# Eight rows of 512 bytes instead of 1,024 single words: the row sums of the spatial weights in a decoder step

## The chip, the cores and the metric

The kernel runs on one core of one Trainium2 chip. The metric is the device time of one execution in microseconds (us). The kernel before was timed in three runs: 998.34 us in the median, 995.13 the lowest and 999.16 the highest.

## The reference, cut to what matters

One decoder layer is computed for 1,024 prompt tokens and 8 sample tokens. A large projection `xn @ w_in` gives seven blocks of 1,024 columns: u, v, z_a, x_b, z_b and the gates g_a and g_b. The change is in branch A, which normalises v and mixes it within chunks of 128 tokens, with one lower-triangular matrix of 128x128 for each of eight groups of channels:

```
u = gelu(u)
vn = layernorm(gelu(v), ln_g, ln_b)                  # per token, over 1,024 channels
w = tril(w_s)                                        # (8, 128, 128): h, t, s
s = einsum('hts,bcshd->bcthd', w, vn) + b_s[h, t]    # per chunk c
y_a = u * s * silu(z_a)
```

The kernel takes gain and bias of the layer norm out of the mixing. With v' the normalised v ahead of gain and bias, channel d of group h has

```
s[t, d] = ln_g[d] * sum_s w[h, t, s] v'[s, d]  +  ln_b[d] * rowsum[h, t]  +  b_s[h, t]
rowsum[h, t] = sum_s w[h, t, s]
```

The 1,024 numbers `rowsum` (8 groups by 128 rows) are what the change stores in another way.

## The kernel before, in words

All products run on TensorE (PE) in fp32r, each as three passes over operands that are cut into a high and a low part. A large product is a Strassen scheme of seven products for each pair of output blocks; one of them takes some 2.8 us. ScalarE (ACT) and VectorE (DVE) cut the weights, form the sums of weights that Strassen needs, and take the results out of PSUM. The stages follow each other in the stream of steps: v, gate A (tiles named ga, garaw, gas, gaw), u and z_a, branch B, gate B, the two merges, the output projection and the embedding gate.

Beside the gate A products the kernel finishes v. `v_planes` cuts the words of each of two v blocks into planes (tiles vw) and turns each with a DMA transpose (`v<-vw`, a pair of them in each call, issued by SyncE, SP); `v_join` puts the turned words together on ScalarE (`big<-v`), and `v_turn` applies gelu. The weights of the next pair of gate blocks are loaded by `Weights.fetch` (two DMAs `garaw`, also on SP).

The functions that the change touches, with the profile's line numbers: `ln_loads` (L938) loads `w_s` into tile ws and the layer norm's gain and bias into the first 16 partitions of tile lnvec. `spatial_weights` (L950) makes ws triangular on GpSimd (POOL), lets VectorE sum its rows (tile rowsums, 128 partitions by 8), stores the sums in DRAM as `rowsum` (8 by 128), turns ws on TensorE (bank psw, 8 transposes) and cuts it, and at last turns lnvec (bank lncol, one transpose) and copies the result to the tile lncol. `spatial_offsets` (L970) loads `rowsum` back, broadcast to all partitions (tile off, 512 KB), and forms the offsets from it, lncol and b_s. `spatial_weights` and `v_planes` are recorded behind the first step of gate A, `ln_loads` three steps into the third pair of v, and `spatial_offsets` behind step 8 of the stream that begins with gate A (L1273 to L1295).

The order of the instructions is not that of the text. All calls behind the start are recorded by `Planner` (L56), which makes the order on every engine. Calls of TensorE in a row into the same tile are one operation of the planner. Each operation depends on those that wrote what it reads, or that read what it writes. Due times are passed backwards (`wanted`, L182): an operation of TensorE is due at its place in the stream of matmuls, and any other operation must end before the earliest due time of the operations that need it. `order` (L204) then takes, engine by engine, the operation that can begin first, and among those that can begin at once the one with the earliest due time, the latter being at most 60 us behind the place where it was recorded. An operation may begin at most 14 us ahead of its due time. In this model each DMA has its bytes and a fixed time to land, whatever its pieces, a store costs SP 0.45 us and a DMA transpose 3 us. SP's DMAs are issued in the order that results, and each waits on SP for its own inputs.

Two resources are shared. There are 46 slots in SBUF for the large tiles (`slot`, L330; lnvec, vw, garaw and gaw each take one), and a new tile takes the slot that was let go first; a load wants three more slots free in the planner. There are two PSUM banks for the small products (`bank`, L339), psw, lncol, vt (the sample's v) and smix (the sample's spatial mix) among them.

In the profile nearly all instructions carry line 299, since the planner issues them there; they are told apart by their tiles.

Of the kernel before, what the change touches and what calls it, by code (L numbers as in the profile page):

```python
# [15 lines left out]
P = 128  # L16
D = 1024
NB = D // P
# [282 lines left out]
@with_exitstack  # L301
def tile_hybrid_step(ctx, tc, *args):
    hybrid_step(ctx, tc, *args)


def hybrid_step(
# [7 lines left out]
    nc = tc.nc  # L314
# [15 lines left out]
    def slot(name, shape=(P, T), dt=F32):  # L330
        n_name[0] += 1
        return plan.tile(spool.tile(list(shape), dt, tag="slot", name=f"{name}_{n_name[0]}", bufs=SLOTS,
                                    padded_shape=None), "slot")
# [5 lines left out]
    def bank(name):  # L339
        n_name[0] += 1  # L340
        return plan.tile(bankp.tile([P, 512], F32, tag="bank", name=f"{name}_{n_name[0]}"), "bank")
# [8 lines left out]
    def split(src, hi, lo):  # L350

        nc.scalar.activation(out=hi, in_=src, func=AF.Copy)
        nc.vector.tensor_tensor(out=lo, in0=src, in1=f32(hi), op=ALU.subtract)

    def dma(out, in_, by=None):
        (by or nc.sync).dma_start(out=out, in_=in_)
# [11 lines left out]
    ident = cpool.tile([P, P], F32, tag="ident", name="ident")  # L368
# [6 lines left out]
    nc = plan  # L375
# [163 lines left out]
    class Features:  # L539

        new = staticmethod(lambda: region("acc"))
        sums = (P, 2, WIDE)
# [15 lines left out]
    class Tokens:  # L558
# [4 lines left out]
        sums = (P, 2, HALF)  # L563
# [366 lines left out]
    lnt = {}  # L930
# [7 lines left out]
    def ln_loads():  # L938
        lnt["ws"] = slot("ws", (P, NB, P))
        dma(lnt["ws"], w_s.rearrange("h t s -> t h s"))  # L940
        vec = lnt["vec"] = slot("lnvec", (P, P))
        for i, v in enumerate((ln_g, ln_b)):
            dma(vec[i * NB : (i + 1) * NB, :], v[0].rearrange("(k p) -> k p", p=P))

    def ln_rows():
        lnt["g"] = row_broadcast(ln_g[0], "lng")
# [3 lines left out]
    def spatial_weights():  # L950

        ws = lnt["ws"]
        nc.gpsimd.affine_select(out=ws, in_=ws, pattern=[[0, NB], [-1, P]], compare_op=ALU.is_ge,
                                fill=0.0, base=0, channel_multiplier=1)
        sums = cpool.tile([P, NB], F32, tag="rowsums", name="rowsums")
        nc.vector.tensor_reduce(out=sums, in_=ws, op=ALU.add, axis=mybir.AxisListType.X)
        dma(kept["rowsum"].rearrange("h t -> t h"), sums)
        lnt["wst"] = []
        for h4 in range(0, NB, 4):
            w = slot("wst", (P, 4, 2, P), F32R)  # L960
            ps = bank("psw")
            for i in range(4):
                nc.tensor.transpose(ps[:, i * P : (i + 1) * P], ws[:, h4 + i, :], ident)
            split(ps.rearrange("p (h t) -> p h t", t=P), w[:, :, 0], w[:, :, 1])
            lnt["wst"].append(w)
        ps = bank("lncol")
        nc.tensor.transpose(ps[:, : 2 * NB], lnt["vec"][: 2 * NB, :], ident[: 2 * NB, : 2 * NB])
        nc.vector.tensor_copy(lncol, ps[:, : 2 * NB].rearrange("p (i k) -> p i k", i=2))

    def spatial_offsets():  # L970

        off = lnt["off"] = slot("off", (P, NB, P))
        dma(off, kept["rowsum"].partition_broadcast(P))
        for h in range(NB):
            nc.vector.scalar_tensor_tensor(out=off[:, h], in0=off[:, h], scalar=lncol[:, 1, h : h + 1],
                                           in1=lnt["bs"][:, h * P : (h + 1) * P], op0=ALU.mult, op1=ALU.add)
# [31 lines left out]
    kept = {}  # L1008
# [262 lines left out]


    at(vsteps[2][3], ln_loads)  # L1273
    at(gasteps[0][0], spatial_weights)
    for i, u in enumerate(vusers):

# [54 lines left out]
    p, l, c = gbsteps[2], gbsteps[3], pasteps[0]  # L1331
    turn_over(yaop, l, [*l[1:], c[0]])
    p, l, c = pasteps[2], pasteps[3], pbsteps[0]
# [414 lines left out]
```

## Time and profile before

| | us |
|---|---|
| median of three runs | 998.34 |
| lowest and highest run | 995.13, 999.16 |
| the profiled execution | 996.61 |
| its span, first to last instruction | 994.9 |
| busy TensorE, share of the span | 979.0, 98% |
| busy VectorE | 797.3, 80% |
| busy ScalarE | 523.4, 53% |
| granted TensorE clock, mean | 0.997 |

A row of the timeline has the start in us from the span's start, the duration, the engine, the line, the operation, the tile written and the tiles read, the size, how many such instructions were merged into the row, and in brackets how long the engine stood idle ahead of it and which releaser ended that. SPq is SP's queue: its rows give the time that SP took to issue DMAs, not the time of the transfer. A row of the table of stretches has the stretch, its length, the busy time of TensorE's matmuls (PE) and weight loads (PEld), VectorE, ScalarE and GpSimd, the granted clock, the DMA share (the mean time that a packet was under way on the 16 DMA engines, over 1 where several were at once) and GB/s. A row of waits has the total in us, how often, and the longest.

### The profile page before, as it was taken

Reading aid. Unit: us, or ns where it says so; the run is one execution under the profiler, and the core shown is the slowest. Engines: PE = TensorE matmul, PEld = TensorE weight load, DVE = VectorE, ACT = ScalarE, POOL = GpSimd, SP = SyncE. Lnnn points to the kernel's source line nnn. Section 1 sums busy time; section 2 is a strip of 40 time slices with the busy share of each in tenths; the row PEclk is TensorE's granted clock in tenths of the full one; section 3 lists DMA queues with packets and bytes.
Section 4 is the critical chain, followed back from the end, with each engine's and each line's share of the span. In section 5 each row is a group of like instructions: output and inputs, shape, how many; then the busy total and the mean of one; then the engine's idle time right before and its main releaser. Section 6 shows DMA issues by size and latency. Waiting matters only on the chain. (4 is left out here: it accounts for less than half of the span.)

```text
span 994.9 us, 15991 instructions
## 1 busy us (share of the span) xinstructions
PE 979.0 (98%) x6110; PEld 878.6 (88%) x6110; DVE 797.3 (80%) x1235; ACT 523.4 (53%) x883; POOL 69.5 (7%) x142
## 2 busy tenths in 40 slices
PE   8999999999999999999999999999999999999996
PEld 6889989999999899899999999999999988888885
DVE  5976558877778888979897987697799898769596
ACT  7778977665434434344533343562353364667463
POOL 2000000000000000001000100000000001213111
PEclk9999999999999999999999999999999999999999
DMA  9325483322464354656735176974663552399546
GB/s 337 133 103 119 116 150 128 101 92 65 143 231 177 106 187 163 215 181 233 254 127 179 29 253 217 305 282 138 227 242 122 178 188 64 88 287 361 157 109 190
DMA packets 106666, 173.48 MB, mean 174 GB/s; under 512 B 25503, under 2 KB 65903, under 8 KB 106582
## 3 DMA queue, kind: packets, MB, share of 16 engines
q1 hardware_dynamic: 104222, 164.56, 49.3%
q0 software_dynamic: 2048, 7.37, 4.2%
q8 instruction: 48, 0.79, 0.3%
q10 hardware_dynamic: 320, 0.54, 0.2%
q14 instruction: 28, 0.23, 0.1%
HBM read 114.84 MB, written 53.87 MB: 170 GB/s over the span
## 5 line engine op out<-in xcount | busy, mean ns | idle before, releaser
L299 DVE TENSOR_TENSOR u<-acc,u 128x520 f32<-128x520 f32 (+1 forms) x90 | 62.6, 695 | 38.0 <-PE acc L299 32.9
L299 POOL TENSOR_TENSOR rstd<-ms,mhalf 128x1 f32<-128x1 f32 (+1 forms) x36 | 30.7, 855 | 190.4 <-DVE ms L299 190.3
L299 POOL MEMSET u<- 128x8 f32 x35 | 4.7, 134 | 503.2 <-PE acc L299 251.0
L299 ACT ACTIVATE u<-acc 128x512 f32<-128x512 f32 x39 | 23.3, 596 | 25.7 <-PE acc L299 25.3
L299 ACT ACTIVATE paw<-pas 128x512 fp32r<-128x512 f32 x16 | 10.0, 627 | 30.3 <-DVE pas L299 25.1
L299 ACT ACTIVATE pbw<-pbs 128x512 fp32r<-128x512 f32 x16 | 10.0, 629 | 26.0 <-DVE pbs L299 23.2
L299 DVE TENSOR_TENSOR big<-big 128x1024 f32<-128x1024 f32 (+4 forms) x20 | 23.6, 1216 | 0.0
L299 ACT ACTIVATE big<-mix 128x256 f32<-128x256 f32 x32 | 12.2, 384 | 19.0 <-PE mix L299 17.1
L299 ACT ACTIVATE big<-v 128x1024 uint16<-128x1024 uint16 x16 | 18.5, 1174 | 6.7 <-DMA v<-vw 6.7
L299 PE MATMUL accm<-qh,wpoolw 128*128 128x260 f32 (+1 forms) x96 | 20.9, 319 | 0.0
L299 ACT ACT_TABLE_LOAD x13 | 16.7, 1283 | 7.0 <-PE acc L299 6.0
L299 ACT ACTIVATE zbw<-zbs 128x512 fp32r<-128x512 f32 x16 | 10.1, 628 | 16.4 <-DVE zbs L299 11.6
L299 ACT ACTIVATE gbw<-gbs 128x512 fp32r<-128x512 f32 x16 | 10.0, 625 | 15.5 <-DVE gbs L299 13.5
L299 DVE TENSOR_TENSOR acc<-acc,u 128x512 f32<-128x512 f32 (+1 forms) x16 | 11.1, 697 | 8.4 <-PE acc L299 8.3
L299 ACT ACTIVATE zaw<-zas 128x512 fp32r<-128x512 f32 x16 | 10.0, 630 | 14.6 <-DVE zas L299 9.1
L299 PEld LDWEIGHTS accm<-qh,wpoolw 128*128 128x128 f32 x96 | 15.6, 188 | 1.9
L299 ACT ACTIVATE uw<-us 128x512 fp32r<-128x512 f32 x16 | 10.0, 626 | 13.4 <-DVE us L299 10.8
L299 DVE TENSOR_TENSOR v<-acc,u 128x520 f32<-128x520 f32 (+1 forms) x9 | 6.3, 697 | 13.3 <-PE acc L299 13.3
L299 ACT ACTIVATE gb<-gb 128x1032 f32<-128x1032 f32 (+1 forms) x8 | 6.8, 854 | 18.8 <-DVE gb L299 18.8
L299 DVE TENSOR_TENSOR big<-mix,big 128x256 f32<-128x256 f32 x32 | 12.7, 419 | 4.8 <-ACT big L299 4.3
L299 ACT ACTIVATE vw<-v 128x1024 uint16<-128x1024 uint16 x16 | 16.1, 1045 | 0.5 <-DVE v L299 0.5
L299 PE MATMUL mix<-wst,vh 128*128 128x256 f32 x64 | 15.5, 319 | 0.0
(685 smaller groups left out, 3623.7 us busy)
## 6 DMA issues: line engine op xcount, KB each, us to landing
ga<-ga SPq DMA_DIRECT2D x16, 516.0 KB
gb<-gb SPq DMA_DIRECT2D x16, 516.0 KB
ya<-za SPq DMA_DIRECT2D x8, 516.0 KB
yb<-zb SPq DMA_DIRECT2D x8, 516.0 KB
x<-in_x_prompt_dram SPq DMA_DIRECT2D x8, 512.0 KB
vraw<-in_w_in_dram SPq DMA_DIRECT2D x8, 512.0 KB
e<-e SPq DMA_DIRECT2D x8, 512.0 KB
garaw<-in_w_in_dram SPq DMA_DIRECT2D x8, 512.0 KB
```

Of the source, the lines that this page charges most:

```text
L299: getattr(getattr(self.nc, e), method)(*args, **kwargs)
```

## The change

`sums` is turned by TensorE in the same bank as lnvec, behind it. VectorE copies the eight rows of 128 sums into a second half of the tile lnvec, which becomes 256 columns wide, and from there they are stored as eight contiguous rows. The store moves from ahead of the psw transposes to the end of the function. The load of `rowsum` in `spatial_offsets` is as before.

```diff
     def ln_loads():
         lnt["ws"] = slot("ws", (P, NB, P))
         dma(lnt["ws"], w_s.rearrange("h t s -> t h s"))
-        vec = lnt["vec"] = slot("lnvec", (P, P))
+        vec = lnt["vec"] = slot("lnvec", (P, 2 * P))
         for i, v in enumerate((ln_g, ln_b)):
-            dma(vec[i * NB : (i + 1) * NB, :], v[0].rearrange("(k p) -> k p", p=P))
+            dma(vec[i * NB : (i + 1) * NB, :P], v[0].rearrange("(k p) -> k p", p=P))
...
         nc.vector.tensor_reduce(out=sums, in_=ws, op=ALU.add, axis=mybir.AxisListType.X)
-        dma(kept["rowsum"].rearrange("h t -> t h"), sums)
         lnt["wst"] = []
...
         ps = bank("lncol")
-        nc.tensor.transpose(ps[:, : 2 * NB], lnt["vec"][: 2 * NB, :], ident[: 2 * NB, : 2 * NB])
+        nc.tensor.transpose(ps[:, : 2 * NB], lnt["vec"][: 2 * NB, :P], ident[: 2 * NB, : 2 * NB])
+        nc.tensor.transpose(ps[:NB, P : 2 * P], sums, ident)
         nc.vector.tensor_copy(lncol, ps[:, : 2 * NB].rearrange("p (i k) -> p i k", i=2))
+        turned = lnt["vec"][:NB, P:]
+        nc.vector.tensor_copy(turned, ps[:NB, P : 2 * P])
+        dma(kept["rowsum"], turned)
```

## The prediction

> **What bounds the kernel now.** I read the head of the page first, then what TensorE (PE) waited for, then TensorE's timeline around its one late wait, and from there backwards through ScalarE (ACT), the queue of SyncE (SP) and the DMA engines, until I came to an operation that the change touches.
>
> ```profile
> span 994.9 us, 15991 instructions
> PE 979.0 (98%) x6110; PEld 878.6 (88%) x6110; DVE 797.3 (80%) x1235; ACT 523.4 (53%) x883; POOL 69.5 (7%) x142
> ```
>
> ```profile
> PE acc L299 <- ACT gaw L299: 2.2, 1, 2.2
> PE warm L299 <- POOL ident masks.py:199: 1.9, 1, 1.9
> ```
>
> TensorE is busy for 98% of the span. The second fence is the head of its list of waits (total, times, longest): the second entry is the warm-up at the very start, and the first is one wait of 2.2 us for a cut of gate weights, gaw. So the kernel is bound by TensorE nearly throughout, and a change can shorten it only by taking matmuls away, by removing that wait, or by letting the matmuls run faster.
>
> ```profile
> 124.09 0.39 PE L299 MATMUL acc<-xB11h,gaw 128*128 128x512 f32 x1
> ...
> 126.85 0.41 PE L299 MATMUL acc<-xB22h,vw 128*128 128x260 f32 x2
> ...
> 145.34 0.66 PE L299 MATMUL smix<-ident,sv 8*128 8x8 f32 x8
> 148.19 0.50 PE L299 MATMUL acc<-xB11h,gaw 128*128 128x512 f32 x1 [2.19 <-ACT gaw L299]
> ...
> 152.87 0.40 PE L299 MATMUL acc<-xB22h,gaw 128*128 128x260 f32 x2
> ```
>
> The first product of the second pair of gate weights should begin when the smix transposes end, at 146.00, and begins at 148.19. It also runs slowly: the same product of the first pair took 126.85 - 124.09 = 2.76 us, this one 152.87 - 148.19 = 4.68 us, 1.92 us more. The last of the stretches below shows why: the granted clock, 1.00 before, is 0.71 from 148 to 150.
>
> ```profile
> 116.00:118.00 2.00, 2.00 (x19) 2.00 (x18) 0.00 (x0) 1.58 (x6) 0.00 (x0) 1.00 1.12 209
> 134.00:136.00 2.00, 2.00 (x10) 1.61 (x9) 1.52 (x6) 2.00 (x5) 0.00 (x0) 1.00 0.78 152
> 136.00:138.00 2.00, 2.00 (x15) 1.87 (x14) 0.97 (x3) 1.97 (x4) 0.54 (x1) 1.00 1.44 68
> 138.00:140.00 2.00, 2.00 (x17) 1.95 (x16) 1.40 (x2) 0.22 (x1) 0.00 (x0) 1.00 1.66 30
> 148.00:150.00 2.00, 1.81 (x5) 1.20 (x6) 1.80 (x6) 2.00 (x6) 0.00 (x0) 0.71 0.08 30
> ```
>
> The last three columns are granted clock, DMA share and GB/s. Why was gaw late?
>
> ```profile
> 117.55 1.18 ACT L299 ACTIVATE big<-v 128x1024 uint16<-128x1024 uint16 x1 [0.42 <-DMA v<-vw]
> ...
> 136.32 1.28 ACT L299 ACT_TABLE_LOAD   x1
> 137.62 0.60 ACT L299 ACTIVATE ga<-acc 128x512 f32<-128x512 f32 x1
> 142.48 2.25 ACT L299 ACTIVATE big<-v 128x1024 uint16<-128x1024 uint16 x2 [4.26 <-DMA v<-vw]
> ...
> 147.52 0.61 ACT L299 ACTIVATE gaw<-garaw 128x512 fp32r<-128x512 f32 x1
> ```
>
> ```profile
> 147.20 0.69 DVE L299 TENSOR_TENSOR gas<-garaw 128x512 f32<-128x512 f32 x1 [3.93 <-DMA garaw<-in_w_in_dram]
> ```
>
> ```profile
> 113.13 4.48 SPq L299 DMA_TRANSPOSE v<-vw  x2
> ...
> 127.96 0.38 SPq L299 DMA_DIRECT2D rowsum<-rowsums  x1
> 133.36 8.21 SPq L299 DMA_TRANSPOSE v<-vw  x2
> 141.68 1.07 SPq L299 DMA_DIRECT2D garaw<-in_w_in_dram  x2
> ```
>
> Two ways lead back to one place. VectorE (DVE) stood idle for 3.93 us until the raw weights garaw landed, whose load SP could issue only at 141.68, behind a pair of DMA transposes. ScalarE stood idle for 4.26 us until the first of these had landed, and still had 147.52 - 142.48 = 5.04 us of work ahead of the cut. This pair held SP for 8.21 us; the earlier pair at 113.13 took 4.48. In the stretches the earlier pair moves 209 GB/s; this one begins at 152 and then falls to 68 and 30 while the DMA share climbs to 1.66: packets wait on something that is not their own bytes. The one DMA between the last good pair and this one that is of another kind is the store of the row sums.
>
> ```profile
> DMA packets 1229, 0.65 MB, mean 185 GB/s; under 512 B 1072, under 2 KB 1072, under 8 KB 1229
> ```
>
> These are the packets between 129 and 132.5 us: 1,024 of the 1,072 small ones are the store's single words. They are read out before 132, but the trace does not show when they are written. I take it that they are still being written one by one and that the transposes behind them on the same engines wait for that. It is an inference: from the order, from the undisturbed pair, and from the rate that falls with no other traffic to explain it.
>
> **The change part by part.** *The scattered store goes.* Its own 0.38 us on SP is no loss or gain, since a store of that kind stays. What goes is the hold-up: the pair would start at 133.36 as now and take some 4.5 us (4.48), so that SP reaches garaw at about 138.0 instead of 141.68. The load needed at most 147.20 - 141.68 = 5.5 us to reach VectorE, so garaw is there at 143.5. ScalarE got the earlier pair's first half 117.55 - 113.13 = 4.42 us after its issue; here that gives 137.8, ScalarE is done with ga at 138.22, and its 5.04 us of work end at 143.3. The cut of gaw (0.61) can run from 143.5 to 144.1, and TensorE wants it at 146.00. The wait of 2.19 us goes, with 1.9 us to spare, and with it the slow stretch, 1.92 us. Next in line is TensorE itself: nothing else in its list is late.
>
> That the slow stretch goes with the gap rests on the clock's rows: 1.00 ahead of the wait, 0.71 directly behind it. [...]
>
> *The added transpose.* `sums` (128x8) is turned by the identity: one more matmul of 128 columns.
>
> ```profile
> 129.72 1.04 PE L299 MATMUL psw<-ident,ws 128*128 128x128 f32 x8
> 130.51 0.48 PE L299 MATMUL acc<-xT2h,gaw 128*128 128x260 f32 x2
> ...
> 133.54 0.23 PE L299 MATMUL lncol<-ident,lnvec 16*128 16x16 f32 x1
> ```
>
> Eight like it take 130.51 - 129.72 = 0.79 us, 0.10 each; a lone one, as lncol is now, lasts 0.23 from start to end. It stands directly on TensorE's path: +0.10, at most +0.23.
>
> *The wait for the sums.* The lncol transposes now need the reduction too. In the planner the reduction had its due time from the far-off offsets, and now has it from this transpose, so VectorE does it no later than now.
>
> ```profile
> 126.72 1.21 DVE L299 TENSOR_REDUCE rowsums<-ws 128x8 f32<-128x1024 f32 x1
> ...
> 133.70 0.70 DVE L299 TENSOR_TENSOR u<-acc,u 128x520 f32<-128x520 f32 x1 [1.43 <-issue]
> 134.32 0.16 DVE L299 COPY lncol<-lncol 128x16 f32<-128x16 f32 x1
> ```
>
> It ends at 127.93, and the transpose runs at 133.54: no wait. If it moves up it costs VectorE 1.21 us there, between nothing (idle time hides it) and 1.21 on TensorE; I take nothing, since VectorE's row at 133.70 alone shows 1.43 us idle.
>
> *The added copy* out of PSUM, 8x128, is near the copy of 128x16 at 0.16 us, behind which VectorE has idle time: nothing, at most some 0.2.
>
> *The store's new place.* It now waits for the copy, so it can be issued from about 134.7 on. If SP takes it ahead of the pair, the pair starts at about 135.2 instead of 133.36, garaw is reached at 139.8 and the cut is done at 145.9: just in time. If SP takes it behind the pair or behind garaw, as its distant due time suggests, nobody waits, since its one reader, the load of the offsets, is planned far behind. Its eight rows write 4 KB, which is nothing beside the transposes.
>
> *The larger vec tile* occupies one slot of the 46 as before, but until the store has been read: from 133.5 to some 142, if SP takes the store behind garaw.
>
> ```profile
> SPq L299 <- DVE gaw L299: 19.4, 3, 10.7
> ```
>
> Between 120 and 180 us SP does wait for slots. The cost lies between nothing and one product (2.76 us) later for garaw; 1.9 of that is covered, so at most about 0.9. I take nothing.
>
> The sum: -2.19 - 1.92 + 0.10 = -4.0 us. The profiled execution took 996.61 us (span 994.9 and 1.7 around it), so the same execution would take 992.6. The runs before went from 995.13 to 999.16 with a median of 998.34, 1.7 above the profiled one. I subtract from the median and get 994.3, -0.40%. If the runs differ through this very wait, the new median lies nearer 992.6.
>
> **The rivals.** *The store is not the cause.* A table load of ScalarE begins at 136.32, just as the rate falls, and something unseen could hold the transposes. For it: the pair's first 2 us run while the store would already be draining. Against it: that load lasts 1.28 us, to 137.60, and from 138 to 140 the rate is lower still. Then only 0.10 us is added: 998.4.
>
> *The slow stretch has another cause and stays* where it is, so that only the gap goes: -2.19 + 0.10, 996.2. For it: TensorE had been busy without a break until 146, and one gap of 2.19 us is not much. Against it: the row from 148 to 150 is the first with a low clock, right behind the gap. [...]
>
> *Another wait takes its place.* A slot comes free one product later and leaves 0.9 us of wait, with or without a slow stretch of 1.92: 995.2 to 997.1. The order of all later work is planned anew, and lists of that kind can move. For it: SP's waits for slots. Against: the margin of 1.9 us.
>
> *Slower: SP is held by the new store.* If it is put ahead of the transposes, and the lncol transposes run later than now, SP waits for TensorE. The point of decision is the pair starting at 141.68 - 4.5 = 137.2, so a copy that ends after about 136.8. Two to three products later (2.76 us each, a copy at about 143) the pair starts at 143.4, garaw is reached 6.2 us later than now, and the sum is +6.2 + 0.1: 1004.6. Against it: the transpose needs nothing that is late, and the transposes' due time is nearer than the store's.
>
> **How the numbers follow.** What a measurement of this kernel can tell from no change is about 0.5%, 5.0 us: faster means under 993.35, slower over 1003.3. The forecast gets 0.70, with a range of its own of 991.5 to 995.5; because of the open question of which execution to subtract from, 0.33 of this lies under 993.35 and 0.37 above. The store not being the cause gets 0.10, the slow stretch staying 0.06, another wait 0.09, all within 0.5%; the held queue 0.05, slower. That makes faster 0.33, same 0.62, slower 0.05. The range leaves out the slower case and the ends and takes in the unchanged time: 991.5 to 998.6.
>
> **What would show it.** Right: some 1,000 fewer packets under 512 B; the pair of transposes behind the row sums holds SP for about 4.5 us and moves over 200 GB/s throughout; garaw is issued near 138 to 140; TensorE's list of waits has no entry for gaw, and the granted clock is 1.00 from 148 to 154. Wrong: a pair that still takes 8 us (the store was not the cause); the gap gone and the clock still low; a new entry of over 1 us in TensorE's waits; or a store that stands ahead of the transposes on SP and waits there.

## The result, and the profile after

The changed kernel took 994.73 us in the median of 8 runs (993.55 to 995.54), the kernel before 998.23 in the median of 8 (995.13 to 999.16): a ratio of 0.9976, 95% interval 0.9965 to 0.9986. In a second set of runs it was 993.88 against 996.71: 0.9966, 0.9954 to 0.9979. The medians are 3.5 and 2.8 us apart; the ratios are not the quotients of the medians, and put the gain at 2.4 and 3.4 us. All of this lies under the 0.5% that the prediction called the least that can be told apart, but both intervals leave out 1. The profiled execution of the changed kernel took 995.54 us; before's took 996.61.

The head of the changed kernel's page:

```profile
span 993.8 us, 15986 instructions
PE 979.9 (99%) x6111; PEld 879.7 (89%) x6111; DVE 796.1 (80%) x1236; ACT 523.9 (53%) x883; POOL 69.6 (7%) x142
...
DMA packets 105642, 173.48 MB, mean 175 GB/s; under 512 B 24471, under 2 KB 64879, under 8 KB 105558
```

The same line of before's page:

```profile
DMA packets 106666, 173.48 MB, mean 174 GB/s; under 512 B 25503, under 2 KB 65903, under 8 KB 106582
```

1,024 packets fewer for the same bytes: the edit does what it says. The changed kernel's list of what TensorE waited for:

```profile
PE warm L299 <- POOL ident masks.py:199: 1.9, 1, 1.9
...
PE acc L299 <- DVE u L299: 1.0, 1, 1.0
...
PE acc L299 <- DVE ga L299: 0.2, 1, 0.2
```

The wait of 2.2 us for gaw, before's longest, is gone; the only wait left near that place is 0.2 us for ga. The queue of SP around the pair of transposes:

```profile
135.07 4.44 SPq L299 DMA_TRANSPOSE v<-vw  x2
140.07 1.00 SPq L299 DMA_DIRECT2D garaw<-in_w_in_dram  x2
141.12 0.40 SPq L299 DMA_DIRECT2D rowsum<-lnvec  x1
141.62 0.46 SPq L299 DMA_DIRECT2D bsb<-in_b_s_dram  x1
```

The pair holds SP for 4.44 us instead of 8.21, and the store stands behind garaw. All times here are some 1.8 us later than in before's profile: this execution lost that much at its start, which is shown further down. The table of stretches:

```profile
136.00:138.00 2.00, 2.00 (x10) 1.65 (x9) 1.42 (x7) 2.00 (x5) 0.00 (x0) 1.00 0.94 182
138.00:140.00 2.00, 2.00 (x16) 1.88 (x16) 1.18 (x3) 1.35 (x7) 0.54 (x1) 1.00 1.15 213
140.00:142.00 2.00, 2.00 (x16) 1.92 (x16) 1.38 (x2) 1.98 (x2) 0.00 (x0) 1.00 1.07 187
...
148.00:150.00 2.00, 1.99 (x16) 1.99 (x17) 1.97 (x7) 1.38 (x4) 0.00 (x0) 1.00 0.00 0
150.00:152.00 2.00, 2.00 (x15) 1.81 (x14) 2.00 (x7) 2.00 (x4) 0.00 (x0) 1.00 0.00 0
```

Where before fell to 68 and 30 GB/s, this holds 182 to 213; and the granted clock stays at 1.00 where it was 0.71. What was not in the sum is a new order of the work on ScalarE, VectorE and TensorE. Their timelines, one after the other:

```profile
139.55 1.19 ACT L299 ACTIVATE big<-v 128x1024 uint16<-128x1024 uint16 x1 [0.65 <-DMA v<-vw]
140.76 1.28 ACT L299 ACT_TABLE_LOAD   x1
142.05 0.60 ACT L299 ACTIVATE ga<-acc 128x512 f32<-128x512 f32 x1
...
146.51 1.13 ACT L299 ACTIVATE gaw<-garaw 128x512 fp32r<-128x512 f32 x2
```

```profile
116.47 1.21 DVE L299 TENSOR_REDUCE rowsums<-ws 128x8 f32<-128x1024 f32 x1
...
136.03 0.27 DVE L299 COPY lnvec<-lncol 8x128 f32<-8x128 f32 x1
```

```profile
147.15 0.66 PE L299 MATMUL smix<-ident,sv 8*128 8x8 f32 x8
148.01 0.51 PE L299 MATMUL acc<-xB22h,gaw 128*128 128x260 f32 x2 [0.20 <-DVE ga L299]
...
150.97 0.40 PE L299 MATMUL acc<-xB11h,gaw 128*128 128x512 f32 x1
```

lnvec's slot is now held until the store has read it, so ga has to take another slot. ScalarE takes ga out behind the first turned block of v (142.05) instead of ahead of it, and TensorE takes another product first (xB22 at 148.01, xB11 only at 150.97). That the slot is the reason is shown below, by the version in which lnvec is let go early; which slot ga takes instead, no view shows. The reduction has moved up by some 12 us (1.8 us of later start taken off) into idle time of VectorE.

**Four executions of the kernel before.** It was profiled three times more, and this says most about the size of the gain. The stretches, what TensorE waited for, and SP's row of the pair, in the second (999.58 us):

```profile
10.00:12.00 2.00, 1.24 (x4) 0.99 (x4) 2.00 (x3) 2.00 (x4) 0.00 (x0) 0.74 1.03 414
12.00:14.00 2.00, 2.00 (x6) 1.52 (x6) 1.41 (x4) 2.00 (x5) 1.27 (x2) 0.50 1.02 354
...
150.00:152.00 2.00, 1.81 (x5) 1.19 (x6) 1.80 (x6) 2.00 (x6) 0.00 (x0) 0.73 0.07 29
152.00:154.00 2.00, 2.00 (x6) 1.59 (x5) 1.94 (x5) 1.97 (x4) 0.00 (x0) 0.50 0.00 0
154.00:156.00 2.00, 2.00 (x14) 1.80 (x13) 1.66 (x4) 1.63 (x6) 0.99 (x1) 0.92 0.00 0
```

```profile
PE acc L299 <- ACT gaw L299: 2.5, 1, 2.5
```

```profile
135.05 8.52 SPq L299 DMA_TRANSPOSE v<-vw  x2
```

The fourth (995.06 us), the same three views:

```profile
148.00:150.00 2.00, 1.54 (x6) 0.98 (x7) 1.53 (x6) 2.00 (x6) 0.00 (x0) 1.00 0.13 49
150.00:152.00 2.00, 2.00 (x12) 1.68 (x11) 1.97 (x6) 1.97 (x4) 0.00 (x0) 1.00 0.00 0
```

```profile
PE acc L299 <- ACT gaw L299: 1.0, 1, 1.0
```

```profile
134.85 6.91 SPq L299 DMA_TRANSPOSE v<-vw  x2
```

The hold-up is there each time, but its length is not the same: 8.21 us in the first, 8.52 in the second, 9.06 in the third (999.37 us, a gap of 2.9 and again 0.50 of the clock from 152 to 154), 6.91 in the fourth. The gap on TensorE follows it: 2.2, 2.5, 2.9, 1.0. Behind the first three gaps the clock is slow; behind the fourth it is not. So the first three executions paid some 4 to 4.6 us (the gap and the 1.7 us that the slow clock costs), the fourth about 1. Why the hold-up varies is told under "When the words landed".

The first two rows of the second execution show another slow stretch, at the span's very start. The first 20 us then take 0.9 to 1.7 us longer; the second, third and fourth execution of before have it and so has the changed kernel's profile, while before's first and the changed kernel's second profile (993.88 us) have not. It belongs to the execution and not to the change. Compared like with like: 999.58 - 995.54 = 4.04 us with it, 996.61 - 993.88 = 2.7 without. But the fourth execution of before, which pays the slow start and hardly any stall, took 995.06, 0.5 less than the changed kernel's 995.54.

### The profile page after: what moved, and what is told of

The parts are those of the page before. It is cut to its first block, busy times and chain, and to the rows that moved or that the text cites. A ratio compares the mean times of both kernels' runs of the same rounds, so it can differ in the third digit from the quotient of the medians.

```text
span 993.8 us, 15986 instructions
## 1 busy us (share of the span) xinstructions
PE 979.9 (99%) x6111; PEld 879.7 (89%) x6111; DVE 796.1 (80%) x1236; ACT 523.9 (53%) x883; POOL 69.6 (7%) x142
## 5 line engine op out<-in xcount | busy, mean ns | idle before, releaser
L299 DVE TENSOR_TENSOR acc<-acc,u 128x512 f32<-128x512 f32 (+1 forms) x16 | 11.2, 700 | 8.2 <-PE acc L299 8.2
```

Source lines behind the costliest of these rows:

```text
L299: getattr(getattr(self.nc, e), method)(*args, **kwargs)
```

## The experiments

Edits are against the kernel before or the changed one, as said. In the kernels that rearrange `rowsum`, the same number of sums is stored, in another order, so the offsets are formed from permuted sums. `before_again`, `before_third` and `before_fourth` are the executions told of above; `after_again` is the second profile of the changed kernel.

> The kernel before once more, with a profile. Theory: the pair of transposes at about 133 us takes 8 us again, TensorE waits some 2.2 us for gaw, and a stretch of 3.4 us at half the clock follows. The clock at the start of the span (a slow stretch of 3.4 us at 11 us in the changed kernel's profile, none in before's) belongs to the execution and not to the kernel, so it may be there or not.

> The kernel before once more, to see what its low runs are (993.4 to 995.6 us, about one in four) beside its high ones (998 to 999). If the hold-up is there in every execution, the pair takes about 8 us again and TensorE waits over 2 us, and low and high differ by the slow stretch at the start (1.7 us) and by small waits alone. If it varies from execution to execution, a low one shows a pair of under 6 us and a wait of under 1 us with no slow stretch behind it, and the gain of the change is an average of executions with and without the stall.

> As for the run ahead of it: another execution of the kernel before, with the same question.

> The changed kernel once more, on the chip of the other three. Theory: 2.5 to 4 us below before. In its first profile the start was 1.8 us longer than in that of before (a slow stretch of the clock at 11 us); if that is chance, this profile's span is nearer 992.

**Fewer, larger pieces at the old place.** Against before:

```diff
-        dma(kept["rowsum"].rearrange("h t -> t h"), sums)
+        dma(kept["rowsum"].rearrange("h t -> (h t)").rearrange("(t h) -> t h", h=NB), sums)
```

> The kernel before with one thing changed: the row sums are stored in the same place, from the same tile, but as 128 runs of 32 bytes (token by group) instead of 1,024 single words. The offsets are then formed from sums in the wrong places. The planner's order is that of before on every engine. Theory (the single words hold the transposes): the pair of transposes behind the store holds SP for about 4.5 us instead of 8.21, garaw is issued near 138, the gap of 2.19 us in front of the second gate A pair and the slow clock behind it go, and the time is 4.1 us below before (ratio 0.996). Rival (the gain of the change comes from the new order or place of the store): the pair still takes some 8 us and the time is that of before.

It took 992.88 us, ratio 0.9955 (0.9943 to 0.9968). SP's queue:

```profile
128.02 0.33 SPq L299 DMA_DIRECT2D rowsum<-rowsums  x1
133.42 4.78 SPq L299 DMA_TRANSPOSE v<-vw  x2
138.30 1.19 SPq L299 DMA_DIRECT2D garaw<-in_w_in_dram  x2
```

Nothing but the pieces of the store (and where each lands in the table) differs from before, the order of all engines is the same, and the whole stall is gone. The store is the cause; the rival that it is not falls. 128 pieces of 32 bytes hold the pair no longer than 4.78 us, so that pieces were as small as 32 bytes was not enough to hold it. Pieces eight times as large are also eight times fewer, and this run can't tell which of the two counted.

**The copy in a place of its own.** Against the changed kernel, with lnvec as small as before:

```diff
-        turned = lnt["vec"][:NB, P:]
+        turned = sv[32 : 32 + NB, :P]
```

> The changed kernel, but the turned sums go to unused partitions of the sample's v tile, so that the slot of the small layer norm tile is let go as early as before. Theory (part of the gain is lost because that slot is held until the store, which puts the gate's evacuation behind a turned v block on ScalarE and moves TensorE's order): TensorE's order is that of before plus one transpose, ScalarE does the gate's evacuation ahead of the joining of v again, and the time is 3.5 to 4.0 us below before, so up to 1 us below the changed kernel. Rival (the slot costs nothing): the same time as the changed kernel.

993.78 us, ratio 0.9971 (0.9954 to 0.9987), beside 0.9966 for the changed kernel on the same chip: no difference. TensorE has before's order again, but for the added transpose, and ScalarE takes ga ahead of the turned blocks, so the slot was the reason for the new order. The slot and the new order cost nothing that can be measured. The expected gain did not come, and the theory that the swap gives something back falls.

**The words in the new place.** Against the changed kernel:

```diff
-        dma(kept["rowsum"], turned)
+        dma(kept["rowsum"].rearrange("h t -> (h t)").rearrange("(t h) -> h t", h=NB), turned)
```

> The changed kernel with its store in the same place of the same order, but as 1,024 single words again (each of the eight rows goes to words that lie 32 bytes apart, so the sums land in the wrong places). Theory: the words no longer stand ahead of the transposes, so these take about 4.5 us and the gap stays away; but the loads behind the store (b_s, and the raw gate weights just ahead of it) are held up for some 10 us, which costs little, as nothing near waits for b_s: within 1 us of the changed kernel. Rival (the words cost wherever they are): a gap of 2 us or more returns and the time is that of before.

999.29 us, ratio 1.0024 (1.0014 to 1.0033): a miss, and the rival's gap came back. What TensorE waited for, SP's queue, then VectorE's and ScalarE's timeline:

```profile
PE acc L299 <- DVE ga L299: 2.2, 1, 2.2
```

```profile
138.56 0.98 SPq L299 DMA_DIRECT2D garaw<-in_w_in_dram  x2
139.59 0.40 SPq L299 DMA_DIRECT2D rowsum<-lnvec  x1
140.09 4.14 SPq L299 DMA_DIRECT2D bsb<-in_b_s_dram  x1
```

```profile
147.08 0.69 DVE L299 TENSOR_TENSOR gas<-garaw 128x512 f32<-128x512 f32 x1 [3.63 <-DMA garaw<-in_w_in_dram]
```

```profile
151.35 1.15 ACT L299 ACTIVATE gaw<-garaw 128x512 fp32r<-128x512 f32 x2 [5.85 <-DMA rowsum<-lnvec]
```

Two things were not foreseen. The first of the two loads of garaw was issued 1.0 us ahead of the words, as early as could be wished, and still came only at 147.08, 8.5 us after its issue (at most 5.5 in before). ga stood in VectorE's queue right behind the sum that waited for it, and TensorE waited 2.2 us for ga. And the tile gaw that ScalarE writes lies in the slot that the store reads from, so it had to wait until the store was done, at 151.35, 11.8 us after its issue. The place behind garaw is no shelter for 1,024 words.

**The same without the shared slot.** Both edits together:

```diff
-        turned = lnt["vec"][:NB, P:]
+        turned = sv[32 : 32 + NB, :P]
...
-        dma(kept["rowsum"], turned)
+        dma(kept["rowsum"].rearrange("h t -> (h t)").rearrange("(t h) -> h t", h=NB), turned)
```

> The version with the turned sums in the sample's v tile, but stored as 1,024 single words in its new place behind the raw gate weights. The run with the words from the layer norm tile had two holds: the last shares of garaw landed late, and ScalarE's cut waited 5.8 us for the slot of that tile, which the store held. Theory (both count): without the slot the cut can run when garaw has landed, near 147, so that a gap of 1 to 2 us stays, and the time is 1 to 3 us below that run, near before. Rival (only the slot held it): no gap, and the time of the changed kernel.

1002.17 us, ratio 1.0066 (1.0042 to 1.009): worse, not better, so the slot was not the main thing. TensorE's wait:

```profile
PE acc L299 <- ACT gaw L299: 5.4, 1, 5.4
```

VectorE and ScalarE again waited for DMAs issued beside the words, in their timelines:

```profile
156.15 0.23 DVE L299 TENSOR_TENSOR smixs<-smixs,bsb 128x64 f32<-128x64 f32 x1 [4.55 <-DMA bsb<-in_b_s_dram]
```

```profile
150.11 0.63 ACT L299 ACTIVATE gaw<-garaw 128x512 fp32r<-128x512 f32 x1 [3.79 <-DMA garaw<-in_w_in_dram]
```

In this order b_s stands in VectorE's queue ahead of the sums for the next product, so a late b_s stops that product. In both runs the load behind the words came late, and so did the second half of garaw, issued some 0.5 us ahead of them.

**Twice the words.** Against before, with a second table:

```diff
         dma(kept["rowsum"].rearrange("h t -> t h"), sums)
+        dma(kept["rowsum2"].rearrange("h t -> t h"), sums)
```

> The kernel before with the scattered store of 1,024 single words made twice, into two tables, one behind the other; the order is otherwise that of before. Theory (single words are written one after the other, some 10 ns each, and what stands behind them waits): the pair of transposes behind them is held for about 10 us more, some 18 us instead of 8.21, garaw is issued near 151, the gap grows from 2.2 to about 12 us, and the time is about 10 us above before (ratio 1.010). Rival (a fixed hold-up, whatever the number of words, or another cause): the time of before.

999.56 us, ratio 1.0033 (1.0018 to 1.0048): 2.3 us more in the median, 3.3 by the ratio, a quarter to a third of the 10 us expected. SP's row of the pair:

```profile
133.59 8.25 SPq L299 DMA_TRANSPOSE v<-vw  x2
```

8.25 us lies within what one store gives (6.91 to 9.06). A hold-up in proportion to the words is not so. Where the 2.3 to 3.3 us come from is open; the runs (997.75 to 1001.55) lack the low ones of before, so perhaps every execution now pays the slow stretch.

**Pieces of 8 bytes.** Against before:

```diff
-        dma(kept["rowsum"].rearrange("h t -> t h"), sums)
+        dma(kept["rowsum"].rearrange("h t -> (h t)").rearrange("(a t w) -> t a w", a=4, w=2),
+            sums.rearrange("t (a w) -> t a w", w=2))
```

> The kernel before with the row sums stored as 512 pieces of 8 bytes, in the wrong places of the table; the order is that of before. Theory (the number of pieces sets the hold-up): half as long, so the writes end some 5 us sooner, near 136, the pair of transposes takes at most 5.5 us, and the gap goes: the time of the version with 128 runs of 32 bytes, 4 us below before. Rival (any piece this small holds as long): a pair of 8 us and the time of before.

993.7 us, ratio 0.9973 (0.9957 to 0.9989). SP's row of the pair and TensorE's wait:

```profile
134.85 5.19 SPq L299 DMA_TRANSPOSE v<-vw  x2
```

```profile
PE acc L299 <- ACT gaw L299: 0.3, 1, 0.3
```

With 512 pieces instead of 1,024 the pair takes 5.19 us instead of 6.91 to 9.06, that is 0.7 us over the undisturbed 4.48 instead of 2.4 to 4.6: less than half. Of TensorE's wait 0.3 us are left, and no slow clock behind it.

**Words to another memory.** Against the kernel with 128 pieces, 1,024 words more, into a tile of SBUF:

```diff
+        apart = cpool.tile([P, NB, 2], F32, tag="apart", name="apart")
+        dma(apart[:, :, 0], sums)
```

> The kernel before with the row sums stored in DRAM as 128 runs of 32 bytes (wrong places), and besides 1,024 single words copied from the same tile into SBUF, in the same place of the order. Theory (it is the writing of small pieces to DRAM that is slow): the words into SBUF hold nothing, the pair of transposes takes about 4.5 us, and the time is 4 us below before. Rival (it is the number of small packets on the DMA engines, wherever they go): a pair of some 8 us and the time of before.

994.99 us, ratio 0.9977 (0.9962 to 0.9992). SP's queue:

```profile
129.44 0.74 SPq L299 DMA_DIRECT2D apart<-rowsums  x1
130.22 0.66 SPq L299 DMA_DIRECT2D rowsum<-rowsums  x1
134.85 4.54 SPq L299 DMA_TRANSPOSE v<-vw  x2
```

As many words, written to SBUF, leave the pair at 4.54 us, which is no hold-up. It is the writing of words to DRAM that holds it: 4.54 us against 8.21.

**The added work alone.** Against before; the store stays 1,024 words:

```diff
+        nc.tensor.transpose(ps[:NB, P : 2 * P], sums, ident)
         nc.vector.tensor_copy(lncol, ps[:, : 2 * NB].rearrange("p (i k) -> p i k", i=2))
+        nc.vector.tensor_copy(sv[32 : 32 + NB, :P], ps[:NB, P : 2 * P])
```

> Before, with only the added work: the sums are turned and copied, and nobody reads the copy; the store stays 1,024 single words from where it was. VectorE's reduction of the sums moves up as in the changed kernel, so that the store is issued earlier, at some 118 to 120 us instead of 127.96. If words being written hold up whatever is near them and are done some 13 us after their issue (141 - 128 in before), they are done by about 133 here, the pair of transposes takes 4.5 to 5 us instead of 8.21, and the time is 3 to 4 us below before (ratio 0.996 to 0.997): the store's place alone would be enough. If the reduction's place does not bring the store forward, or the words hold the pair wherever they stand, the time is that of before + 0.1 (ratio 1.000).

993.17 us, ratio 0.9971 (0.9956 to 0.9987). SP's queue:

```profile
113.00 4.56 SPq L299 DMA_TRANSPOSE v<-vw  x2
117.61 0.81 SPq L299 DMA_DIRECT2D rowsum<-rowsums  x1
...
133.52 4.71 SPq L299 DMA_TRANSPOSE v<-vw  x2
138.34 1.40 SPq L299 DMA_DIRECT2D garaw<-in_w_in_dram  x2
```

The same words, unchanged, are stored 10 us earlier, because the added transpose gives the reduction an earlier due time. They then have 15.9 us until the pair, in which SP issues only two loads, and the pair takes 4.71 us. The whole gain is there without any larger piece. The orders on VectorE and ScalarE are not quite those of before (they are those of the version with the copy in a place of its own), so the place of the store is not all that differs.

**When the words landed.** In the traces the landing of a DMA shows as counts on a semaphore, 16 for the store of the sums, each with its time, though no view lists them one by one. In us, from the issue on SP to the last count:

| run | the store of the sums | the pair's first transpose |
|---|---|---|
| before, first to fourth execution | 13.1, 13.3, 13.8, 11.9 | 9.1, 9.4, 9.8, 7.9 |
| 128 pieces of 32 bytes | 3.8 | 5.0 |
| 512 pieces of 8 bytes | 6.1 | 5.1 |
| 1,024 words to SBUF | 4.7 | 4.5 |
| twice 1,024 words | 12.3 and 12.4 | 8.5 |
| 1,024 words, 10 us earlier | 12.8 (10 of 16 counts kept) | 5.0 |
| 1,024 words behind garaw, two runs | 11.7, 11.2 | 4.5, 4.5 |
| the changed kernel | 4.8 | 4.5 |

The words to DRAM took 11.2 to 13.8 us to land wherever their store stood. In the four executions of before the first held transpose is down 1.4 to 1.5 us behind the last word, and the longer the words take, the longer the pair holds SP: 6.91 us with 11.9, 9.06 with 13.8. So the length of the stall follows that of the words' landing, which differs from execution to execution. Two stores of 1,024 words landed together in the time of one (12.3 and 12.4 us), so here the time did not grow with the number of words of this size. In the run with the added work alone the words are as slow as ever, and something beside them is late there too: the two loads behind them (lng and lnb) land 7.4 and 8.1 us after their issue instead of about 4 and 5 in before. No engine waits for these, and that is why the place alone is enough.

## Why the prediction was right, point by point

*The cause.* Right, and now shown, where the prediction called it an inference: the hold-up goes away with larger pieces (128 of 32 bytes), with another memory (SBUF) and with distance (15.9 us). The order on every engine is that of before in the first two, but for the one added store; in the third VectorE and ScalarE have a new order. The prediction said that the trace does not show when the words are written. Its views don't, but the counts do: the words were landing until 141.04, as the prediction took it, and the transposes were down right behind them. That they are written "one by one" is not borne out, since twice the words took no longer (12.3 and 12.4 us against 11.9 to 13.8). Why words of 4 bytes land so slowly stays open.

*The pair and garaw.* 4.44 us against 4.48 expected. garaw at 140.07, less the 1.8 us of this execution's start, is 138.3 against 138.0. The rate was to be over 200 GB/s throughout; it was 182 to 213.

*The gap of 2.19 and the slow stretch of 1.92.* Both gone, together; of the 1.92 the clock's own rows account for 1.7. The rival in which the slow stretch stays falls: behind gaps of 2.2 to 2.9 us the clock was slow (three executions of before, the words in the new place, twice the words), behind 1.0 and 0.3 it was not, and without a gap never at this place. The prediction's "nothing else in its list is late" was not quite so: before's list has waits of 1.2, 1.0 and 0.8 us elsewhere in the span. They stay in the changed kernel and don't touch the sum.

*The added transpose.* 0.10 expected. Matched matmul by matmul (the start of each in one trace against the start of the same one in the other), the changed kernel loses 0.11 us at this place against each of the four executions of before.

*The reduction, the copy, the store.* The reduction moved up into idle time and cost nothing, as taken. The copy took 0.27 us rather than 0.16, behind no one's wait. The store went behind garaw, one of the two places that were called free. That a moved reduction would also move a store was not thought of; in the changed kernel the store waits for the copy and it did not matter.

*The larger vec tile.* Nothing was taken, at most 0.9 for a garaw one product later. It did change the slots, by another way: ga was late, and TensorE swapped two products. It cost 0.2 us of wait, and the version without it is no faster.

*The sum.* That 994.73 came so near to 994.3 is in part luck: the mechanism was right, but a stall read in one execution was taken off a median of others. Matched matmul by matmul, the changed kernel's first profile gains 4.1 us at the stall against before's second execution and ends 4.1 ahead. Its second profile, against before's first, gains 3.8 there and ends 2.8 ahead, since it lost 0.6 in the first 20 us, 0.1 at the added transpose and 0.3 in small steps later. Its first profile, against before's fourth, gains 1.0 at the stall and ends 0.4 behind: 0.3 lost ahead of the stall and 1.1 in steps of 0.1 to 0.4 over the rest of the span. Such steps belong to executions as much as to kernels: before's second execution loses 1.1 us on its first in two of them, at 592 and 771 us. So the terms -2.19 and -1.92 were about right where they were read and wrong as constants: the stall is of another length in each execution, and where the gap is 1.0 us the second term is nought. That the medians differ by 3.5 and 2.8 us instead of 4.0 fits this, as far as four executions can show it. The prediction's aside, that the median would lie nearer 992.6 if the runs differ through this wait, had the premise half right and the conclusion wrong: before's runs differ through the slow start too, and the changed kernel's runs have that start in one profile and not in the other.

*The slower rival*, SP held by the store ahead of the transposes, did not come. Its neighbour, which no one named, is dearer: words behind garaw, at 999.29 and 1002.17 us.

## What to carry to other kernels

Here a store of 1,024 single words to DRAM took SP 0.38 us to issue in before, and 11.2 to 13.8 us to land over the runs, and transfers issued behind it, sometimes also the one just ahead, came late: in before the first transpose landed 7.9 to 9.8 us after its issue instead of 4.5, with the added work alone lng and lnb 7.4 and 8.1 instead of about 4 and 5, and the second half of garaw, ahead of the words with no shared slot, 9.6 instead of 4.9 in before. Look for a falling rate at a high DMA share behind such a store (68 and 30 GB/s at 1.44 and 1.66 in before). Make the pieces larger, or place it where no load that is soon needed stands near: each of these alone gave the whole gain (ratios 0.9955 and 0.9971). Before subtracting a stall from a median, profile the same kernel a few times: here the stall cost 4 to 4.6 us in three executions, with a slow clock behind gaps of 2.2 to 2.9, and about a quarter of that in the fourth, with a gap of 1.0 and no slow clock.

## What the runs showed of the hardware that was not expected

A gap of 2.5 us on TensorE was followed by 3.4 us at half the clock: in before's second execution the stretches from 150 on have 0.73, 0.50 and 0.92, which is 0.54 + 1.00 + 0.16 = 1.70 us lost, half of 3.4. Behind the gap of 5.4 us, in the kernel with the words behind garaw and no shared slot, the slow stretch is twice as long; the first and the last row of its table of stretches, with three at 0.50 between them:

```profile
156.00:158.00 2.00, 0.00 (x0) 0.00 (x0) 1.78 (x7) 2.00 (x6) 0.00 (x0) 0.81 0.00 0
...
164.00:166.00 2.00, 2.00 (x11) 1.66 (x10) 1.89 (x6) 1.75 (x7) 0.91 (x1) 0.98 0.83 257
```

0.38 + 3.00 + 0.04 = 3.42 us, or 6.8 us at half the clock, of which the first 1.4 pass before the matmuls resume at 158.67. In before's first execution, 0.71 from 148 to 150 is 1.16 us at half the clock, so by this estimate the slow stretch began near 148.8, some 0.6 us after the matmuls had resumed at 148.19: in this execution the clock dropped neither with the gap nor at its end. At the start of the span the same two gaps, 1.19 and 0.77 us, were followed by a slow stretch in some executions and not in others (0.74 and 0.50 from 10 to 14 in before's second, 1.00 in its first); no run here shows why.

The words held up transfers issued ahead of them as well: garaw, 1.0 us earlier on the queue, came 8.5 us after its issue (at most 5.5 in before). Not always: with no shared slot, the first half of garaw, 1.1 us ahead of the words, landed in 4.7 us, and the second half, 0.6 ahead, in 9.6. And SP itself stood at the next DMA behind them, 4.14 us at a load of b_s that takes 0.46 in the changed kernel.
